# Two more feature tiles in the seven-product groups, and values left without their token scale

## The chip, the core and the metric

The program runs on one core of one Trainium2 chip. Five engines matter: TensorE (PE: matmuls, with PEld for its weight loads), VectorE (DVE), ScalarE (ACT), GpSimd (POOL) and the sync engine (SP), which only issues DMAs here. Every engine takes its own instructions strictly in the order in which the kernel was written and waits on semaphores of the others. The metric is the device time of one execution in microseconds, as the median of the runs of a kernel.

## The reference

The block has a token-mixing half and a feed-forward half, for 256 tokens of width 2048 in float32. The change is in the feed-forward half:

```python
def _rmsnorm(x, g):
    y = xf * lax.rsqrt(jnp.mean(xf * xf, axis=-1, keepdims=True) + EPS)
    return (y * g.astype(jnp.float32)).astype(x.dtype)

def _conv_ffn(h, w_up, dw_w, dw_b, w_down):
    up = h @ w_up
    gate, val = up[..., :D_FF], up[..., D_FF:]
    gate = lax.conv_general_dilated(gate, dw_w, ...) + dw_b
    act = jax.nn.gelu(gate, approximate=False) * val
    return act @ w_down

x = x + _conv_ffn(_rmsnorm(x, norm2_g), w_up, dw_w, dw_b, w_down)
return _rmsnorm(x, normf_g)
```

D_FF is 5504, that is 43 feature tiles of 128. The convolution runs over neighbouring tokens (width 3), for each feature by itself. The last line normalizes every token (row) of x by its own root mean square.

## The kernel before

**Precision.** Every float32 operand of a matmul is split into a high part (`hi`, rounded to the type that TensorE takes in one pass) and the rest (`lo`). ACT makes `hi` by a copy (L197 for weights as loaded, L1129 for the weights of the seven products), DVE makes `lo` by subtracting (L205, L1130). A product is then three matmuls: high by high, high by low, low by high. The `hi` and `lo` buffers of weights are three deep.

**Items.** `ff_items` writes out by hand the order of the feed-forward half, as a list of items. There are 43 gate and 43 value units ("u", written g36 or v36 here for tile 36), each the up-projection of one tile by `still_weights` (L372): 16 matmuls of 512 columns and 16 of 256. There are products ("s"), late downs ("d") and four `last` units. The strings in `PATTERNS` give the order, one string for each group. `ff_step(n)` runs beside item n on PE: it runs the list `beside[n]`, then `split_item(n + 2)`, which splits the weights of the item two further on, and then the list `behind[n]`. What a unit leads to is entered into these lists by `up_posts`: the eviction and sum one item later (`scaled_sum`: ACT copies the low part out of PSUM at L1013, DVE adds at L1015 and multiplies by `r2b`, the row of token scales, at L1016), the convolution (`gate_conv`, L1023 to L1027) and the value product (`val_mult`) two items later.

**The down-projection in three ways.** Tiles in groups go by seven products in place of eight: with the tokens in two halves, the tiles of a group in two halves and the output columns in two halves (n), the 2x2 block product is made from seven block products of sums and differences, named P1, P7, N5, N3, P6, P2, N4, for each of two column blocks c. A group of `(first, m)` holds 2m tiles; each of its 14 products is 3m matmuls of 512 columns (`by_parts`, L1232 to L1234). There are five groups with 36 tiles: one of 4 and four of 8. P1 and N5 gather in four held PSUM banks (`held`) over all groups, P6 and P7 in SBUF tiles `Z` and P2, N3 and N4 in the residual `xs` (`product_out`); `shared_out` adds what is shared at the end, in three steps. Tiles 36 to 39 (`LATE`) are multiplied directly, as four late downs over 512 output columns each (`moving_weights`, L355 to L357); tiles 40 to 42 (`LAST`) come at the end, as eight products of nine matmuls.

In the last group P2 and N4 of each c are not evicted: their banks stay in `joined` until the late down of the same c has added to them, and `down_out` (L1239) adds them to `xs`. The products and units other than the held ones take turns in the four banks of the pool `mm`.

**The weights of the products.** For each group and c four blocks a, b, c, d of the down weights arrive through a ring of two tiles (`rawd`), loaded by SP's queue; the split of P1, P7, N3 and P2 loads the next one. A further tile `x`, called `sumw` in the trace, holds sums: `first_sums` (L1144) makes a + b on DVE, and a DMA that adds while it writes puts d onto b. N5 splits sumw; then such a DMA adds d to it (L1134), P6 splits it; another adds c (L1136), N4 splits it. The adding DMAs are issued by POOL.

**Scales.** `r2b` first holds the two columns of the token norm's reciprocal root; `row_out` turns them and writes them to memory and `row_in` reads them back as a row over all partitions, so that a feature tile (features by tokens) can be multiplied by it. At the end the sums of squares of the residual with EPS give the last norm's scale (`first_squares`, L1245).

Of the kernel before, what the change touches and what calls it, by code (L numbers as in the profile page):

```python
# [11 lines left out]
ALU = mybir.AluOpType  # L12
# [6 lines left out]
NH = 12  # L19
# [7 lines left out]
EPS = 1e-6  # L27
# [14 lines left out]
V_N = 216  # L42
# [35 lines left out]
OUT_ORDER += [(c, k) for c in (2, 3) for k in range(4)]  # L78


GROUPS = [(0, 2), (4, 4), (12, 4), (20, 4), (28, 4)]
LATE = list(range(36, 40))
LAST = list(range(40, NF))
PRODUCTS = [
    ["P1", "P7", "N5", "N3", "P6", "P2", "N4"], ["P1", "N5", "P7", "N3", "P6", "P2", "N4"]
# [1 line left out]


PATTERNS = ["uuu" + "su" * 13 + "s"] * (len(GROUPS) - 1)
PATTERNS += ["uuu" + "su" * 6 + "sdu" + "ssu" * 2 + "suuss" + "ddd"]  # L90


def group_of(j):

    for g, (first, n) in enumerate(GROUPS):
        if j < first + 2 * n:
# [4 lines left out]
def ff_items():  # L101
# [4 lines left out]

    firsts = [first for first, _ in GROUPS] + [LATE[0], NF]
    items = ups(0, firsts[1])
# [12 lines left out]
def block_kernel(  # L121
# [19 lines left out]
    nc = tc.nc  # L141
# [7 lines left out]
    def f32(ap):  # L149
        return ap.bitcast(F32)  # L150
# [5 lines left out]
    units = [(w_u_x[i], 2048) for i in range(4)] + [(w_in[i], 2048) for i in range(20)]  # L156
# [4 lines left out]
    for n, it in enumerate(items):  # L161
        if it[0] == "product":
            continue
        up_index[n] = len(units)
        if it[0] in ("gate", "val"):
            units.append((w_up[2 * it[1] + (it[0] == "val")], 2048))
            shifts.append((0, SHIFT))
            continue
        elif it[0] == "down":
            units.append((w_down_late[it[1]], 2048))  # L170
        else:
            units.append((w_down_last[it[1]], 512 * len(LAST)))
        shifts.append((0, 0))
# [25 lines left out]
    def split_low(i, o=0, n=2048, reload=True):  # L199

        if i >= len(units):
            return
        hi, lo = halves[i]
        s = slice(o, min(o + n, units[i][1]))
        nc.vector.tensor_tensor(lo[:, s], raws[i][:, s], f32(hi[:, s]), ALU.subtract)  # L205
        if s.stop == units[i][1] and reload:
            load(i + RAW)
            load_more(i + RAW)
# [80 lines left out]
    ps = bank(dn, "ps_warm")  # L289
# [3 lines left out]
    def vcol(o, n=1):  # L293
        return vec[:, o : o + n]
# [25 lines left out]
    def row_out(t, name):  # L320

        nc.vector.transpose(t[:, 32:64], t[:, 0:32])
        row = rows.tile([2, 4, 32], F32, tag="row" + name, name="row" + name)
        for b in range(2):
            nc.sync.dma_start(row[b], t[b:P:32, 32:64])
        return row
# [80 lines left out]
    for c in range(4):  # L407
        t = base.tile([P, 4, 512], F32R, tag=f"hT{c}", name=f"hT{c}")
        hT.append(t)
    ps_u = [bank(mm, f"ps_u{b}") for b in range(2)]  # L410
    for k in range(NK):
# [3 lines left out]
        n = 1 if c < 2 else 2  # L415
# [3 lines left out]
        if q % n == 0:  # L419
            w, h = u_part(k, 0, FW, n), hi[:, q : q + n, :]  # L420
# [512 lines left out]
    def flip_x_in(c):  # L933
        t = turned_tiles(c)[1]
        t = st["x", c] = t.rearrange("p (k c) -> p k c", k=4)
        blocks_in(st.pop(("d", "x")), t)
# [19 lines left out]
    for n, (c, kq) in enumerate(OUT_ORDER):  # L956
# [15 lines left out]
        if kq >= 2:  # L972
            part = "a" if kq == 2 else "f"
            ps = ps_a[c] if kq < 3 else ps_a[c, "f"]
# [16 lines left out]
    fp = ctx.enter_context(tc.tile_pool(name="fp", bufs=2))  # L991
    hT[:] = hT2
    r2b = fp.tile([P, S], F32, tag="r2b", name="r2b", bufs=1)
    parts = {}
    gate_out, sums_of, act = {}, {}, {}

# [14 lines left out]
    def scaled_sum(ps, name):  # L1011
        tmp = fp.tile([P, S], F32, tag="ftmp", name=f"ft_{name}")
        nc.scalar.activation(tmp, ps[:, S : 2 * S], AF.Copy)  # L1013
        add = fp.tile([P, S], F32, tag="fadd", name=f"fa_{name}", bufs=3)
        nc.vector.tensor_tensor(add, ps[:, 0:S], tmp, ALU.add)  # L1015
        nc.vector.tensor_tensor(add, add, r2b, ALU.mult)  # L1016
        sums_of[name] = add

    def gate_conv(j):
# [17 lines left out]
    def val_mult(j):  # L1037
        va, ge = sums_of.pop(f"v{j}"), gate_out.pop(j)
        if j >= LATE[0]:
            q = j - LATE[0]  # L1040
            if q % 2 == 0:
# [30 lines left out]
    def block_of(g, name):  # L1072
        k, t = PLACE[name]
        return parts[g, k][:, 0 : GROUPS[g][1], t * P : (t + 1) * P]

    def operand(g, name):

        o = fp.tile([P, 2, 4, P], F32R, tag=f"op_{name}", name=f"op_{name}", bufs=1)
        o = o[:, :, 0 : GROUPS[g][1], :]
        a = block_of(g, name)  # L1080
# [15 lines left out]

    ring, ring_tiles = [(g, c, w) for g in range(len(GROUPS)) for c in range(2) for w in "abdc"], {}
    ring_next = [0]
# [97 lines left out]
    def product_out(g, c, p, ps):  # L1196
        tt = nc.vector.tensor_tensor
        if p in ("P6", "P7"):
            z = Z[c, p]
            if g == 0:  # L1200
                nc.scalar.activation(z, ps, AF.Copy)
            else:
                tt(z, ps, z, ALU.add)
        else:
            n, t = {"P2": (0, 0), "N3": (1, 0), "N4": (0, 1)}[p]
            xb = xs[2 * n + c][:, t, :]
            tt(xb, ps, xb, ALU.add)

    def shared_out(c, step):

        p1, n5, u, p7 = held[c, "P1"], held[c, "N5"], Z[c, "P6"], Z[c, "P7"]
        x00, x10, x01, x11 = (xs[2 * n + c][:, t, :] for n in range(2) for t in range(2))
        tt = nc.vector.tensor_tensor
        if step == 0:
            tt(u, p1, u, ALU.add)
            tt(x00, p1, x00, ALU.add)
            w = st["w", c] = wp.tile([P, 512], F32, tag="junk", name=f"sum01_{c}")
            tt(w, n5, u, ALU.subtract)
        elif step == 1:
            tt(u, u, p7, ALU.add)  # L1220
            tt(x01, x01, st["w", c], ALU.add)
            tt(x10, x10, u, ALU.add)
        else:
            w = st.pop(("w", c))
            tt(w, w, p7, ALU.subtract)
            tt(x11, x11, w, ALU.add)

    def by_parts(ps, o, hi, lo, n, first, last):

# [12 lines left out]
    ssq3 = base.tile([P, 2, 32], F32, tag="ssq3", name="ssq3")  # L1242

    def first_squares(b):
        nc.vector.tensor_scalar(ssq3[:, b, 3:4], ssq3[:, b, 0:1], EPS, None, ALU.add)  # L1245

    ready = {(c, b): xs[c][:, b, :] for c in range(4) for b in range(2)}

# [49 lines left out]
    def last_out_post(c, part, ps):  # L1298

        i = n_front + 2  # L1300
        out_add(c, part, ps)
        flip_x_out(c)
        for o, n in ((0, 512), (512, 1536)):
            split_low(i - 1, o, n)
        out_sums(c)
        split_high(i)
        split_low(i, 0, 1024)
        tot2 = base.tile([P, 2], F32, tag="tot2", name="tot2")
        nc.vector.tensor_reduce(tot2, ssq2, mybir.AxisListType.X, ALU.add)
        rstd_of(tot2, D, "2", r=r2b[:, 0:2])  # L1310
        split_low(i, 1024, 1024, reload=False)
        row = row_out(r2b, "2")
        flip_x_in(c)
        row_in(row, r2b)
        load(i + RAW)
# [4 lines left out]
    for q in range(OPEN):  # L1320
        kind, j = items[q]
        ps = bank(mm, f"ps_{kind}{j}")
# [29 lines left out]
    for n, it in enumerate(items):  # L1352
        if n < OPEN:
            continue
        if it[0] == "last":
            break
        if n in (4, 5):
            ring_load()
        if n == 6:
            pending.append(lambda: first_sums(0, 0))  # L1360
        if it[0] in ("gate", "val"):
            kind, j = it
            ps = bank(mm, f"ps_{kind}{j}")
            still_weights(*halves.pop(up_index[n]), ps, range(NK))
            ff_step(n)
            up_posts(n, kind, j, ps)
            continue
        if it[0] == "product":
            kind, g, c, p = it
            end = g == len(GROUPS) - 1  # L1370
            if (c, p) in held:
                by_parts(held[c, p], parts[p], *halves.pop(it), GROUPS[g][1], g == 0, end)
            elif end and p in ("P2", "N4"):
                ps = joined[c, p] = bank(mm, f"ps_{p}{g}{c}")
                by_parts(ps, parts[p], *halves.pop(it), GROUPS[g][1], True, False)
            else:
                ps = bank(mm, f"ps_{p}{g}{c}")
                by_parts(ps, parts[p], *halves.pop(it), GROUPS[g][1], True, True)
                at(beside, n + 1, product_out, g, c, p, ps)
            if end and p == ("N4", "P6")[c]:  # L1380
                for q in range(3):
                    at(behind, n + 1 + (1 + c) * q, shared_out, c, q)
        else:
            kind, c = it
            hi, lo = halves.pop(up_index[n])
            if c < 2:
                ps = [joined.pop((c, p)) for p in ("P2", "N4")]
            else:
                ps = [bank(mm, f"ps_l{c}{b}") for b in range(2)]
            for b in range(2):  # L1390
                moving_weights(hi, lo, 512, LATE, act.get, b, ps[b], c >= 2, True)
            at(beside, n + 1, down_out, c, ps)
            if c == 1:
                gfb = fp.tile([P, D], F32, tag="sumw", name="gfb", bufs=1)
                nc.gpsimd.dma_start(gfb, normf_g.partition_broadcast(P))
        ff_step(n)
# [165 lines left out]
```

## Time and profile before

| | us |
|---|---|
| median of 3 runs (lowest, highest) | 933.49 (933.27, 934.07) |
| the profiled execution's own time | 933.83 |
| its span in the trace | 932.1 |
| busy in it: PE, DVE, ACT, POOL | 923.2, 776.2, 543.6, 62.8 |

The time of an execution holds a little more than the span from the first to the last instruction in the trace. A row of a group reads: line, engine, operation, output and inputs, shapes, count, then busy time in us and the mean duration of one in ns, then the idle time of the engine before them with what ended it. A row of the timeline starts with the start in us from the span's start and the duration. A row of waits ends with the sum, the count and the longest in us. Matmuls are pipelined, so the distance between the starts of two of them, and not the duration of one, is what it costs.

### The profile page before, as it was taken

The page shows a single profiled execution, that of the slowest core. Times are in us where ns is not written, and L with a number is a line of the kernel's source. Part 1 is how long each engine was busy: PE and PEld are TensorE (multiplying, and loading weights), DVE is VectorE, ACT ScalarE, POOL GpSimd, SP SyncE. Part 2 cuts the span into 40 slices and gives each one's busy share as a digit, 9 for nine tenths or more (in the row PEclk, how much of TensorE's full clock was granted, in tenths as well). Part 3 has the DMA queues.
Part 4 walks back from the last instruction along what each step waited for, and adds up shares of the span by engine and source line. Part 5 has one row for each costly group of instructions (what it writes and reads, how often), then busy time and mean ns, then how long its engine had stood idle before and what let it go on. Part 6 is the DMA issues. An engine that isn't in the chain of part 4 may idle for free.

```text
span 932.1 us, 12883 instructions
## 1 busy us (share of the span) xinstructions
PE 923.2 (99%) x4973; PEld 799.9 (86%) x4973; DVE 776.2 (83%) x997; ACT 543.6 (58%) x689; POOL 62.8 (7%) x79
## 2 busy tenths in 40 slices
PE   9999999999999999999999999999999999999996
PEld 7888998888888888888888888888888888888885
DVE  7768998787768877898877997888978789989995
ACT  6756777546465655565555665555755556655553
POOL 0101111200000000000000000000000000000002
PEclk9999999999999999999999999999999999999999
DMA  9865777667777668788797769887787968779652
GB/s 361 331 225 158 249 241 215 201 198 269 230 274 256 203 207 256 242 274 263 229 299 251 240 209 298 223 260 233 268 240 244 306 221 269 237 238 272 203 180 91
DMA packets 59597, 225.16 MB, mean 242 GB/s; under 512 B 24465, under 2 KB 30225, under 8 KB 35984
## 3 DMA queue, kind: packets, MB, share of 16 engines
q1 hardware_dynamic: 54928, 194.72, 57.9%
q0 software_dynamic: 4464, 29.36, 17.0%
q8 instruction: 39, 0.64, 0.3%
q10 hardware_dynamic: 144, 0.26, 0.1%
q14 instruction: 22, 0.18, 0.0%
HBM read 216.98 MB, written 7.08 MB: 240 GB/s over the span
## 4 chain that ended last, share of the span: by engine, by line
PE 98%; DMA 0%; ACT 0%; DVE 0%; issue 0%; POOLq 0%; POOL 0%; ACTq 0%
PE ps_gate L372 25%; PE ps_val L372 25%; PE ps_q L372 7%; PE ps_P L1233 4%; PE ps_P L1234 4%; PE ps_P L1232 3%; PE ps_N L1233 3%; PE ps_N L1234 3%; PE ps_N L1232 3%; PE ps_k L372 2%; PE ps_a L357 2%; PE ps_a L355 2%; PE ps_a L356 2%; PE ps_s L748 1%; PE ps_o L842 1%; PE ps_ff L355 1%
## 5 line engine op out<-in xcount | busy, mean ns | idle before, releaser
L205 DVE TENSOR_TENSOR lo<-raw,hi 128x2048 fp32r<-128x2048 f32 (+2 forms) x133 | 295.0, 2221 | 28.3 <-ACT hi L197 28.0
L197 ACT ACTIVATE hi<-raw 128x2048 fp32r<-128x2048 f32 (+1 forms) x131 | 246.8, 1887 | 27.6 <-PE ps_a L356 10.8
L372 PE MATMUL ps_gate<-hU,hi 128*128 128x512 f32 x688 | 236.1, 389 | 0.0
L372 PE MATMUL ps_val<-hU,hi 128*128 128x512 f32 x688 | 236.1, 389 | 0.0
L372 PE MATMUL ps_gate<-hU,lo 128*128 128x256 f32 x688 | 189.9, 276 | 0.0
L372 PE MATMUL ps_val<-hU,lo 128*128 128x256 f32 x687 | 189.6, 276 | 0.0
L372 PEld LDWEIGHTS ps_gate<-hU,hi 128*128 128x128 f32 x688 | 129.2, 188 | 26.8
L372 PEld LDWEIGHTS ps_val<-hU,hi 128*128 128x128 f32 x688 | 129.2, 188 | 26.8
L372 PEld LDWEIGHTS ps_gate<-hU,lo 128*128 128x128 f32 x688 | 129.2, 188 | 1.3
L372 PEld LDWEIGHTS ps_val<-hU,lo 128*128 128x128 f32 x687 | 129.0, 188 | 1.3
L1013 ACT ACTIVATE ft_g<-ps_gate 128x256 f32<-128x256 f32 x43 | 16.5, 384 | 121.1 <-PE ps_gate L372 121.1
L1013 ACT ACTIVATE ft_v<-ps_val 128x256 f32<-128x256 f32 x43 | 16.5, 383 | 87.0 <-PE ps_val L372 87.0
L372 PE MATMUL ps_q<-hT,hi 128*128 128x512 f32 x192 | 65.0, 391 | 0.0
L1232 PE MATMUL ps_P<-hi_P,op_P 128*128 128x512 f32 x144 | 56.0, 389 | 0.0
L1233 PE MATMUL ps_P<-hi_P,op_P 128*128 128x512 f32 x144 | 56.0, 389 | 0.0
L1234 PE MATMUL ps_P<-lo_P,op_P 128*128 128x512 f32 x144 | 56.0, 389 | 0.0
L372 PE MATMUL ps_q<-hT,lo 128*128 128x256 f32 x192 | 51.2, 277 | 0.0
L1130 DVE TENSOR_TENSOR lo_N<-sumw,hi_N 128x2048 fp32r<-128x2048 f32 (+1 forms) x20 | 41.5, 2076 | 9.4 <-ACT hi_N L1129 9.2
L1232 PE MATMUL ps_N<-hi_N,op_N 128*128 128x512 f32 x108 | 42.0, 389 | 0.0
L1233 PE MATMUL ps_N<-hi_N,op_N 128*128 128x512 f32 x108 | 42.0, 389 | 0.0
L1234 PE MATMUL ps_N<-lo_N,op_N 128*128 128x512 f32 x108 | 42.0, 389 | 0.0
L372 PEld LDWEIGHTS ps_q<-hT,hi 128*128 128x128 f32 x192 | 35.2, 188 | 6.6
(415 smaller groups left out, 1592.4 us busy)
## 6 DMA issues: line engine op xcount, KB each, us to landing
raw<-in_w_up SPq DMA_DIRECT2D x86, 1024.0 KB, 6.6
raw<-in_w_in SPq DMA_DIRECT2D x20, 1024.0 KB, 5.4
raw<-in_w_out SPq DMA_DIRECT2D x16, 1024.0 KB, 5.1
sumw<-in_w_down POOLq DMA_DIRECT2D x16, 1024.0 KB, 8.6
raw<-in_w_down_late SPq DMA_DIRECT2D x4, 1024.0 KB, 6.8
raw<-in_w_down_last SPq DMA_DIRECT2D x4, 768.0 KB, 4.0
turnp<-flip SPq DMA_DIRECT2D x44, 64.0 KB, 1.9
flop<-turnp SPq DMA_DIRECT2D x11, 256.0 KB, 3.9
```

The lines of the kernel that those rows point to most:

```text
L197: nc.scalar.activation(halves[i][0][:, s], raws[i][:, s], AF.Copy)
L205: nc.vector.tensor_tensor(lo[:, s], raws[i][:, s], f32(hi[:, s]), ALU.subtract)
L355: nc.tensor.matmul(ps, ah, wh, start=first and q == q0, stop=False)
L356: nc.tensor.matmul(ps, al, wh, start=False, stop=False)
L357: nc.tensor.matmul(ps, ah, wl, start=False, stop=last and q == q0 + len(kk) - 1)
L372: nc.tensor.matmul(ps[:, x], (hi, lo)[i][:, k * P : (k + 1) * P], hk(k)[:, x], start=n == 0 and k == 0, stop=n == len(order) - 1 and k == ...
L748: nc.tensor.matmul(ps[:, b * S : (b + 1) * S], qT[:, qo + b * P : qo + (b + 1) * P], kT[:, ko : ko + S], start=n == 0, stop=n == 2,)
L1013: nc.scalar.activation(tmp, ps[:, S : 2 * S], AF.Copy)
L1130: nc.vector.tensor_tensor(lo, src, f32(hi), ALU.subtract)
L1232: nc.tensor.matmul(ps, o[:, 0, p, :], hi[:, s], start=first and p == 0, stop=False)
L1233: nc.tensor.matmul(ps, o[:, 1, p, :], hi[:, s], start=False, stop=False)
L1234: nc.tensor.matmul(ps, o[:, 0, p, :], lo[:, s], start=False, stop=last and p == n - 1)
```

## The change

38 tiles go through the groups: the first group has 6 tiles in place of 4, so that all later groups begin two tiles on, and the late set has two tiles in place of four, with late weights of 1024 columns in place of 2048. The last group's pattern has fewer units, and its products come two at a time from the start. The gate keeps its multiplication by `r2b`, the values lose theirs. So what the down-projection gives is larger by the token's root mean square (`rms2`, the reciprocal of the scale); the residual is multiplied by `rms2` when the first group's products are added to it (one of its four parts in `shared_out`), and EPS of the last norm is multiplied by its square (`eps3`), so that the last norm, which takes out any factor of a token, gives the same. The ring's first loads and the first sums begin at items 8, 9 and 10 in place of 4, 5 and 6.

```diff
-GROUPS = [(0, 2), (4, 4), (12, 4), (20, 4), (28, 4)]
-LATE = list(range(36, 40))
+GROUPS = [(0, 3), (6, 4), (14, 4), (22, 4), (30, 4)]
+LATE = list(range(38, 40))
...
 PATTERNS = ["uuu" + "su" * 13 + "s"] * (len(GROUPS) - 1)
-PATTERNS += ["uuu" + "su" * 6 + "sdu" + "ssu" * 2 + "suuss" + "ddd"]
+PATTERNS += ["uuu" + "ssu" * 3 + "sdu" + "ssu" * 3 + "s" + "ddd"]
...
-            units.append((w_down_late[it[1]], 2048))
+            units.append((w_down_late[it[1]], 512 * len(LATE)))
...
+    rms2, eps3 = vcol(V_N + NH, 2), vcol(V_N + NH + 2, 2)
...
         nc.vector.tensor_tensor(add, ps[:, 0:S], tmp, ALU.add)
-        nc.vector.tensor_tensor(add, add, r2b, ALU.mult)
+        if name[0] == "g":
+            nc.vector.tensor_tensor(add, add, r2b, ALU.mult)
...
-            tt(xb, ps, xb, ALU.add)
+            if g == 0:
+                nc.vector.scalar_tensor_tensor(xb, xb, rms2[:, t : t + 1], ps, ALU.mult, ALU.add)
+            else:
+                tt(xb, ps, xb, ALU.add)
...
-            tt(x11, x11, w, ALU.add)
+            nc.vector.scalar_tensor_tensor(x11, x11, rms2[:, 1:2], w, ALU.mult, ALU.add)
...
-        nc.vector.tensor_scalar(ssq3[:, b, 3:4], ssq3[:, b, 0:1], EPS, None, ALU.add)
+        nc.vector.tensor_scalar(
+            ssq3[:, b, 3:4], ssq3[:, b, 0:1], eps3[:, b : b + 1], None, ALU.add
+        )
...
+        nc.vector.reciprocal(rms2, r2b[:, 0:2])
         row = row_out(r2b, "2")
+        nc.vector.tensor_tensor(eps3, rms2, rms2, ALU.mult)
+        nc.vector.tensor_scalar(eps3, eps3, EPS, None, ALU.mult)
...
-        if n in (4, 5):
+        if n in (8, 9):
             ring_load()
-        if n == 6:
+        if n == 10:
             pending.append(lambda: first_sums(0, 0))
```

## The prediction

> **What bounds the kernel now.** I read the page first, then the waits of TensorE, then its timeline.
>
> ```profile
> span 932.1 us, 12883 instructions
> PE 923.2 (99%) x4973; PEld 799.9 (86%) x4973; DVE 776.2 (83%) x997; ACT 543.6 (58%) x689; POOL 62.8 (7%) x79
> PE 98%; DMA 0%; ACT 0%; DVE 0%; issue 0%; POOLq 0%; POOL 0%; ACTq 0%
> ```
>
> ```profile
> PE ps_warm L291 <- POOL ones L283: 1.0, 1, 1.0
> PE ps_u L429 <- ACT hT L298: 0.2, 1, 0.2
> ```
>
> PE is busy for 99% of the span, carries 98% of the chain that ended last, and after the first microseconds waits for nobody. So a matmul taken away shortens the kernel by its own length, DVE time taken away buys nothing, and any new PE wait is paid in full. The length of a matmul is its pitch, not its modelled duration:
>
> ```profile
> 747.21 0.39 PE L372 MATMUL ps_val<-hU,hi 128*128 128x512 f32 x1
> ...
> 752.65 0.39 PE L1232 MATMUL ps_P<-hi_P,op_P 128*128 128x512 f32 x1
> ...
> 755.37 0.39 PE L372 MATMUL ps_gate<-hU,hi 128*128 128x512 f32 x1
> ```
>
> The first column is the start, the second the modelled duration. An up unit ("u", one gate or value tile) takes 752.65-747.21 = 5.44 us, a four-tile product ("s") 2.72 us for 12 matmuls, so 0.2267 us each.
>
> **The saved matmuls.**
>
> ```profile
> L1232 PE MATMUL ps_P<-hi_P,op_P 128*128 128x512 f32 x144 | 56.0, 389 | 0.0
> L1232 PE MATMUL ps_N<-hi_N,op_N 128*128 128x512 f32 x108 | 42.0, 389 | 0.0
> L355 PE MATMUL ps_l<-hi,act 128*128 128x512 f32 x16 | 6.2, 389 | 0.0
> L1016 DVE TENSOR_TENSOR fa_v<-fa_v,r2b 128x256 f32<-128x256 f32 x43 | 18.3, 425 | 1.5
> ```
>
> Products: (144+108) x 3 lines = 756 matmuls for 36 tiles, 21 a tile. Late: ps_l is half of the column blocks, 16 x 3 = 48, so 96 for 4 tiles, 24 a tile. Two tiles moved: +42-48 = -6 matmuls, **-1.36 us**. The removed value scaling is 18.3 us of DVE; by the waits above it is worth 0 by itself.
>
> **Edits worth nothing.** New small operations and the row of scales:
>
> ```profile
> L787 DVE RECIPROCAL ex<-sm 128x2 f32<-128x2 f32 x12 | 1.9, 155 | 0.0
> L330 SPq DMA_DIRECT2D r2b<-row x1: 332/332/332, 258.0 to 258.0; - x1
> 265.49 0.42 DVE L1016 TENSOR_TENSOR fa_g<-fa_g,r2b 128x256 f32<-128x256 f32 x1
> ```
>
> The reciprocal delays the row's way out by 0.16 us; it is read back at 258.0 and first used at 265.49, which hides it (without that cover: 0.16 us). The two eps3 operations follow the row; eight scalar_tensor_tensor for tensor_tensor cost some 0.06 us each (0.48 against 0.42 in rows below). Group 0 with three tiles has 2.04 us of product to a 5.44 us unit, 7.48; DVE then needs about 2.20+1.66+0.60+1.3 = 5.8, so it stays hidden, as the tighter four-tile groups do now. Ring loads start four items later beside units that start four items later: nothing.
>
> **The new order of the last group.** Before, products and units alternate (s u s u) for its first half c=0. Now two products follow each other: after the last group's own last unit, v37, come N4 (of the group before), g38, v38, g39, P1, P7, v39, N5, N3, g40, P6, P2, v40, N4, down0, g41, P1, N5, v41, P7, N3, g42, P6, P2, v42, N4, down1, down2, down3, last. A down now is 12 matmuls, 2.72 us. So PE has 10.88 us where it had 16.32 from N5 to P6 and from P6 to N4. These three read one tile, sumw: N5 splits it into hi and lo, then POOL's DMA adds d, P6 splits it, a DMA adds c, N4 splits it.
>
> ```profile
> 799.43 2.29 DVE L1130 TENSOR_TENSOR lo_N<-sumw,hi_N 128x2048 fp32r<-128x2048 f32 x1
> ```
>
> ```profile
> 802.01 0.88 POOL L1134 DMA_DIRECT2D sumw<-in_w_down  x1 [29.15 <-DVE lo_N L1130]
> ```
>
> ```profile
> DMA to landing us min/median/max: 8.0/8.5/10.1
> ```
>
> ```profile
> 812.69 0.38 ACT L1013 ACTIVATE ft_v<-ps_val 128x256 f32<-128x256 f32 x1 [2.22 <-PE ps_val L372]
> 812.97 1.91 ACT L1129 ACTIVATE hi_P<-sumw 128x2048 fp32r<-128x2048 f32 x1
> ```
>
> ```profile
> 814.91 2.29 DVE L1130 TENSOR_TENSOR lo_P<-sumw,hi_P 128x2048 fp32r<-128x2048 f32 x1 [0.92 <-ACT hi_P L1129]
> ```
>
> One link, from the end of one lo to PE's start on the next: 0.29 to the issue (801.72 to 802.01), 8.5 landing, 0.05, hi to lo 1.95 (812.97 to 814.91), lo 2.29: **13.08 us**. 16.32 covers it, 10.88 does not. I take the median landing of these last groups; its bounds are 8.0 and 10.1.
>
> DVE's pitches, from stretches where it runs without a gap:
>
> ```profile
> 835.98 2.29 DVE L1144 TENSOR_TENSOR sumw<-rawd41a,rawd41b 128x2048 f32<-128x2048 f32 x1
> 838.18 0.42 DVE L1058 TENSOR_TENSOR act<-fa_v,act 128x256 fp32r<-128x256 f32 x1
> 838.52 0.42 DVE L1015 TENSOR_TENSOR fa_g<-ps_gate,ft_g 128x256 f32<-128x256 f32 x1
> 838.97 0.42 DVE L1016 TENSOR_TENSOR fa_g<-fa_g,r2b 128x256 f32<-128x256 f32 x1
> 839.39 2.29 DVE L205 TENSOR_TENSOR lo<-raw,hi 128x2048 fp32r<-128x2048 f32 x1
> 841.60 0.48 DVE L1024 SCALAR_TENSOR_TENSOR cv<-fa_g,vec,cv 128x255 f32<-128x255 f32 x1
> ...
> 842.52 2.29 DVE L1130 TENSOR_TENSOR lo_P<-rawd41a,hi_P 128x2048 fp32r<-128x2048 f32 x1
> ```
>
> ```profile
> 895.35 2.29 DVE L205 TENSOR_TENSOR lo<-raw,hi 128x2048 fp32r<-128x2048 f32 x1
> 897.55 0.69 DVE L1225 TENSOR_TENSOR sum<-sum,z_P 128x512 f32<-128x512 f32 x1
> 898.27 0.69 DVE L1226 TENSOR_TENSOR xs<-xs,sum 128x512 f32<-128x512 f32 x1
> 898.88 0.68 DVE L1239 TENSOR_TENSOR xs<-ps_P,xs 128x512 f32<-128x512 f32 x1
> ```
>
> ```profile
> L205 DVE TENSOR_TENSOR lo<-raw,hi 128x1536 fp32r<-128x1536 f32 x5 | 8.7, 1754 | 1.2 <-ACT hi L197 1.2
> L205 DVE TENSOR_TENSOR lo<-raw,hi 128x1024 fp32r<-128x1024 f32 x4 | 4.8, 1221 | 0.1
> L1129 ACT ACTIVATE hi_N<-sumw 128x1024 fp32r<-128x1024 f32 x4 | 4.2, 1050 | 0.0
> ```
>
> lo or first sums 2.20; 128x256 steps 0.34 to 0.45 (sum 0.45, gate sum and scale 0.81, conv pair 0.90, act or value product 0.34); 128x512 steps 0.60, a dependent pair 1.32; lo of 1536 and 1024 columns 1.66 and 1.13 (duration less the 0.09 of overlap). A lo behind a unit's eviction starts 2.43 us after the unit: 0.20 (tail of a matmul, 0.39-0.23, and a semaphore), 0.28 and 1.95. PE starts 0.05 after the lo it needs. An item's split is issued two items ahead and its buffer frees three items back.
>
> I set PE's clock to 0 where v37 starts and carry it on.
> (a) **N5 to P6.** g39 ends at 24.48. lo v39 starts at 26.91; then 2.20, operand sums 1.32, operand N5 0.60, act 0.34, conv 0.90, lo N5 2.29: ready at 34.56, due at 35.36. P6 is ready at 34.56+13.08 = 47.64 and due at 46.24: **1.40** (0.46 of it shows before g40, whose lo waits in the same queue: from lo N5's start at 32.27 come 2.20+0.60+0.60+2.20+0.60+0.45+2.29+0.05 = 41.26, due 40.80).
> While ACT waits for sumw, hi P2, the eviction of g40, hi v40 and conv 40 are queued behind it, and on DVE their partners.
> **P6 to N4.** P6's lo had ended at 47.59: N4 is ready at 60.67, due at 47.64+10.88 = 58.52: **2.15**.
> (b) **DVE behind the late N4.** From lo N4's start at 58.33 DVE has in its queue: lo N4 2.20, down0's lo 1.13, first sums 2.20, sum of v40 0.45, lo g41 2.20, value product 0.34, lo P1 2.20, act 0.34, three shared steps 1.80, two down additions 1.20, lo N5 2.20, three more shared steps 1.80, gate sum and scale 0.81, lo v41 2.29: 21.16, v41 ready at 79.54. PE is through N4, down0, g41, P1, N5 at 60.67+16.32 = 76.99: **2.55**, most of it before v41.
> (c) **down2's bank.** c=1 has a unit more between N5 and P6, so that link fits. v41 ends at 84.98; P6's lo ends 2.43+2.20+0.34+0.60+2.29 later, 92.84; N4 is ready at 105.92 and due at 95.86+10.88 = 106.74, 0.82 to spare. But its lo starts only at 103.58, and before the bank is free DVE does lo N4 2.20, shared steps 1.80, lo down1 1.13, sum 0.45, lo down2 1.13, shared steps 1.80, value product 0.34, lo down3 1.13, act 0.34 and the first down addition 0.69: 114.59. Of the four mm banks, down2's second is the one that P2 of c=1 held until that addition (before, it was down3's first). PE reaches it at 106.74+2.72+2.72+1.36 = 113.54: **1.10**.
> (d) **Last units.** From 114.50 DVE does the other down addition 0.60, lo of last0 1.66, the dependent pair 1.32, down2's additions 1.20 and lo of last1 1.75, done at 121.03, due at 120.76 (114.64+1.36+2.72+2.04): 0.32 with the 0.05; then last2 1.66, down3's additions 1.20 and last3 1.75 from 119.28+1.66, done at 125.55 against 125.16 (121.08 and two products of nine matmuls, 2.04 each): 0.44. Together **0.76**.
>
> Sum of waits 1.40+2.15+2.55+1.10+0.76 = 7.96; less 1.36: **+6.60 us**. Other DMAs moved: d and c of c=0 are asked for by SP after the lo of P1 and P7 (about 18 and 24) and read at 33 and 45; POOL's addition to b goes out near 6.8 and P7 reads at 19.5, 12.7 us for a landing of 10.1 at most: hidden. POOL has nothing else in its queue there.
>
> The same chain worked for before, with 16.32 us per link, gives no wait, as the trace has none. DVE was near its limit even so:
>
> ```profile
> 774.00:801.00 27.00, 27.00 (x153) 23.59 (x152) 25.80 (x33) 17.79 (x21) 0.00 (x0) 1.00 0.76 250
> ```
>
> 25.80 of 27.00 us (fourth column) in this group's first stretch. The profiled execution took 933.83 us (span 932.1), 0.3 us over the median 933.49; the sum goes on the median: **940.1 us**.
>
> **Rivals.** A: **sumw lands in time**, not slower by the measure. If a landing takes 6.35 us or less (13.08-8.5+6.35 = 10.93, less 0.05), no link holds PE. For it: a plain ring load of this size landed in 6.0:
>
> ```profile
> rawd41b<-in_w_down SPq DMA_DIRECT2D x1, 1024.0 KB, 6.0
> ```
>
> Against it: no addition to sumw here landed under 8.0. Left are 0.46 at g40, 1.34 at v41 (v40's end + 2.43, then b's list from lo g41 on, 15.18, and 0.05, against 16.32 of PE), 0.25 at the bank (v42's end, 0.48 and 1.09 to down2's lo, then 1.13+1.80+0.34+1.13+0.34+0.69+0.05, against 2.72+2.72+1.36) and 0.76: 2.81, net +1.45, **934.9**. The Trainium skill (DMA: Bandwidth & Descriptors, Anatomy of one DMA) fits GpSimd-issued transfers with 2.0 us plus bytes over 436 GB/s, an estimate of 4.4 us for 1 MiB; by that the sum would be this rival's. The trace does not agree: 8.0 to 10.1.
>
> B: **the count alone**. PE stays without a gap, -1.36, **932.1**. It decides only if besides A's landing DVE takes up A's other 2.81 us too, 1.34 of them over five items; 25.80 of 27.00 speaks against that.
>
> C: **landings at the upper bound**, 10.1, since DMAs are packed closer. Each 0.1 costs 0.3 (two links, and the bank by way of N4): 7.96+4.8 = 12.8, net +11.4, **944.9**. For it: the 10.1 happened, at half the density of products. Against: the landing quoted above for N5 to P6 belongs to a stretch with DVE and DMA as full as this one will be. The Trainium skill (SBUF — State Buffer, SBUF: two separate sides) warns that a GpSimd-issued DMA can be starved of descriptors while VectorE holds the port that they share; here the issue took 0.88 us beside a nearly gapless DVE, so no run here shows it.
>
> **Chances.** Forecast 0.75, C 0.09, A 0.08, B 0.05, and 0.03 for a gain over 0.2% from something unseen. A measurement here tells 0.2% (1.87 us) from no change; A and B lie within it. So slower 0.84, same 0.13, faster 0.03. The range reaches from A's 934.9 to C's 944.9; the forecast's own is 938.6 (landing 8.0: 7.96-1.5-1.36 = +5.1) to 941.9 (landing 9.1, +8.4).
>
> **What would show it.** Right: 798 product and 48 late matmuls; PE waits for lo_P and lo_N with ACT's hi waiting for the landing in sumw, about 3.5 us over two places of the last group, 2.5 about v41, 1 at ps_l. The first three quarters of the feed-forward keep 8.16 us per pair. Wrong: PE without waits (B), waits on DVE alone (A), or waits in group 0 or at the opening, which nothing above foresees.

## The result, and the profile after

The changed kernel took **943.96 us** (median of 4 runs, 943.12 to 944.73) against 933.38 (933.25 to 934.07) for the kernel before on the same chip: a ratio of **1.011, 95% interval 1.0094 to 1.0126**, slower. The forecast was 940.1. A later group of runs of the same changed kernel, told below, gave 942.06 and a ratio of 1.0082 (1.0062 to 1.0101). Some executions of the kernel before and of experiments 1, 5, 7 and 8 took some 16 us longer, at the same granted clock (0.996 to 0.999); they are left out, and the medians below are of the others.

The profiled execution took 944.18 us. From its page: the span, the busy times, the chain that ended last and two groups of product matmuls.

```profile
span 942.4 us, 12827 instructions
...
PE 925.5 (98%) x4967; PEld 798.0 (85%) x4967; DVE 763.4 (81%) x955; ACT 545.5 (58%) x687; POOL 62.5 (7%) x79
...
PE 80%; DVE 7%; DMA 7%; issue 3%; ACT 2%; SPq 1%; POOL 0%; POOLq 0%; DVEq 0%; ACTq 0%
...
L1239 PE MATMUL ps_P<-lo_P,op_P 128*128 128x512 f32 x152 | 59.4, 391 | 0.9 <-DVE lo_P L1132 0.8
...
L1239 PE MATMUL ps_N<-lo_N,op_N 128*128 128x512 f32 x114 | 44.5, 390 | 1.2 <-DVE lo_N L1132 1.2
```

PE has six matmuls fewer (4967 against 4973), (152 + 114) x 3 = 798 of them in products, and DVE 12.8 us less work. But PE's share of the chain fell from 98% to 80%: DVE, DMA and the issue of instructions now stand on the path. Who PE waited for, in the view of its waits (sum, count, longest):

```profile
PE ps_val L372 <- DVE lo L205: 2.8, 3, 1.7
PE ps_e L1422 <- DVE lo L205: 1.6, 2, 0.9
PE ps_N L1239 <- DVE lo_N L1132: 1.2, 1, 1.2
PE ps_warm L291 <- POOL ones L283: 1.0, 1, 1.0
PE ps_P L1239 <- DVE lo_P L1132: 0.8, 1, 0.8
PE ps_gate L372 <- DVE lo L205: 0.3, 1, 0.3
```

Every new wait is for a low half made by DVE. The view counts the idle time of PE alone; what is lost is the distance between the starts of two matmuls less the pitch of 0.2267 us. PE's timeline around the last group's first P6 and N4:

```profile
843.26 0.40 PE L1238 MATMUL ps_P<-hi_P,op_P 128*128 128x512 f32 x1
844.49 0.50 PE L1239 MATMUL ps_P<-lo_P,op_P 128*128 128x512 f32 x1 [0.83 <-DVE lo_P L1132]
844.83 0.39 PE L1237 MATMUL ps_P<-hi_P,op_P 128*128 128x512 f32 x1
...
856.17 0.39 PE L1238 MATMUL ps_N<-hi_N,op_N 128*128 128x512 f32 x1
857.76 0.50 PE L1239 MATMUL ps_N<-lo_N,op_N 128*128 128x512 f32 x1 [1.19 <-DVE lo_N L1132]
```

The two matmuls with the high weights run at once and the third, the first that reads the low half, waits: 844.49 - 843.26 - 0.23 = 1.00 us, and 0.11 more to the next start, 1.11 for P6. Added up in this way over the whole timeline, PE loses:

| place | changed kernel, first profile | second profile | forecast |
|---|---|---|---|
| second unit's value at the opening, 252 us | 1.46 | 0 | 0 |
| g40, P6 (and P2, v40 behind it), N4 of c=0 | 0.25, 1.11, 0.83, 1.46 | 0.25, 1.24, 0.83, 1.27 | 3.55 in all |
| g41, v41 | 0.57, 1.98 | 0.63, 1.95 | 2.55 |
| late downs | 0.15 | 0.29 | 1.10 |
| last units | 2.16 | 2.12 | 0.76 |

The kernel before loses nothing after its first microseconds. Behind the last matmul there is one more loss, in what is called the drain below. The span before ended 8.0 us after the start of the last matmul (924.08 to 932.1), here 9.1 (933.29 to 942.4): +1.1.

The links of the chain by way of sumw are on POOL's and ACT's timelines, POOL's issue of the adding DMA and ACT's first read of what it wrote:

```profile
831.28 0.88 POOL L1136 DMA_DIRECT2D sumw<-in_w_down  x1 [25.56 <-DVE lo_N L1132]
844.73 0.88 POOL L1138 DMA_DIRECT2D sumw<-in_w_down  x1 [12.58 <-DVE lo_P L1132]
```

```profile
840.19 1.92 ACT L1131 ACTIVATE hi_P<-sumw 128x2048 fp32r<-128x2048 f32 x1 [6.04 <-DMA sumw<-in_w_down]
853.46 1.92 ACT L1131 ACTIVATE hi_N<-sumw 128x2048 fp32r<-128x2048 f32 x1 [4.47 <-DMA sumw<-in_w_down]
```

From issue to first read are 8.91 and 8.73 us, and ACT stands still for the last 6.04 and 4.47 of them. Then DVE, from the late N4 on, has no gap (its timeline, rows left out between):

```profile
855.41 2.29 DVE L1132 TENSOR_TENSOR lo_N<-sumw,hi_N 128x2048 fp32r<-128x2048 f32 x1 [3.34 <-ACT hi_N L1131]
857.62 1.22 DVE L205 TENSOR_TENSOR lo<-raw,hi 128x1024 fp32r<-128x1024 f32 x1
858.75 2.28 DVE L1146 TENSOR_TENSOR sumw<-rawd41a,rawd41b 128x2048 f32<-128x2048 f32 x1
...
871.55 0.68 DVE L1225 TENSOR_TENSOR z_P<-z_P,z_P 128x512 f32<-128x512 f32 x1
...
874.15 2.29 DVE L205 TENSOR_TENSOR lo<-raw,hi 128x2048 fp32r<-128x2048 f32 x1
```

The row at 874.15 is the low half of v41. PE's wait for it ended at 876.49, 21.08 us after 855.41; the list worked out in the prediction gave 21.16 plus 0.05.

### The profile page after: what moved, and what is told of

Its sections match the earlier page's. It is cut to its first block, busy times and chain, and to the rows that moved or that the text cites. A ratio compares the mean times of both kernels' runs of the same rounds, so it can differ in the third digit from the quotient of the medians.

```text
span 942.4 us, 12827 instructions
## 1 busy us (share of the span) xinstructions
PE 925.5 (98%) x4967; PEld 798.0 (85%) x4967; DVE 763.4 (81%) x955; ACT 545.5 (58%) x687; POOL 62.5 (7%) x79
## 4 chain that ended last, share of the span: by engine, by line
PE 80%; DVE 7%; DMA 7%; issue 3%; ACT 2%; SPq 1%; POOL 0%; POOLq 0%; DVEq 0%; ACTq 0%
PE ps_val L372 23%; PE ps_gate L372 23%; PE ps_q L372 7%; PE ps_P L1237 3%; PE ps_P L1239 3%; PE ps_P L1238 3%; DMA sumw<-in_w_down 3%; PE ps_k L372 2%; PE ps_N L1237 2%; PE ps_N L1239 2%; PE ps_N L1238 2%; DVE lo L205 2%; PE ps_s L748 1%; PE ps_o L842 1%; PE ps_a L357 1%
## 5 line engine op out<-in xcount | busy, mean ns | idle before, releaser
L205 DVE TENSOR_TENSOR lo<-raw,hi 128x2048 fp32r<-128x2048 f32 (+2 forms) x133 | 290.7, 2188 | 31.3 <-ACT hi L197 30.8
L197 ACT ACTIVATE hi<-raw 128x2048 fp32r<-128x2048 f32 (+2 forms) x131 | 243.5, 1860 | 25.2 <-PE ps_a L356 9.9
L1239 PE MATMUL ps_P<-lo_P,op_P 128*128 128x512 f32 x152 | 59.4, 391 | 0.9 <-DVE lo_P L1132 0.8
L1237 PE MATMUL ps_P<-hi_P,op_P 128*128 128x512 f32 x152 | 59.2, 389 | 0.0
L1238 PE MATMUL ps_P<-hi_P,op_P 128*128 128x512 f32 x152 | 59.1, 389 | 0.0
L1132 DVE TENSOR_TENSOR lo_N<-sumw,hi_N 128x2048 fp32r<-128x2048 f32 (+1 forms) x20 | 43.6, 2182 | 18.7 <-ACT hi_N L1131 18.7
L1239 PE MATMUL ps_N<-lo_N,op_N 128*128 128x512 f32 x114 | 44.5, 390 | 1.2 <-DVE lo_N L1132 1.2
L1238 PE MATMUL ps_N<-hi_N,op_N 128*128 128x512 f32 x114 | 44.4, 389 | 0.0
L1237 PE MATMUL ps_N<-hi_N,op_N 128*128 128x512 f32 x114 | 44.3, 389 | 0.0
L1131 ACT ACTIVATE hi_N<-sumw 128x2048 fp32r<-128x2048 f32 (+1 forms) x20 | 36.5, 1824 | 7.8 <-DMA sumw<-in_w_down 7.8
```

Of the source, the lines that this page charges most:

```text
L197: nc.scalar.activation(halves[i][0][:, s], raws[i][:, s], AF.Copy)
L1131: nc.scalar.activation(hi, src, AF.Copy)
L1132: nc.vector.tensor_tensor(lo, src, f32(hi), ALU.subtract)
L1237: nc.tensor.matmul(ps, o[:, 0, p, :], hi[:, s], start=first and p == 0, stop=False)
L1238: nc.tensor.matmul(ps, o[:, 1, p, :], hi[:, s], start=False, stop=False)
L1239: nc.tensor.matmul(ps, o[:, 0, p, :], lo[:, s], start=False, stop=last and p == n - 1)
```

## The experiments

Each is an edit of the changed kernel, but for the first, which is an edit of the kernel before, and the last, which has no edit. All ratios are to the kernel before.

**1. The values without their scale, alone.** The edits of `r2b`, `rms2` and `eps3` on the kernel before, the groups, patterns and late weights of which stay.

```diff
-        nc.vector.tensor_tensor(add, add, r2b, ALU.mult)
+        if name[0] == "g":
+            nc.vector.tensor_tensor(add, add, r2b, ALU.mult)
...
```

> The kernel before, with the values unscaled and the residual multiplied (the rms2 and eps3 part of the change alone; groups, pattern and ring as before). Theory (the loss sits in the new order of the last group, the scale part is worth nothing): 933.4 us, between 932.8 and 934.2, TensorE without a wait after the first microseconds. Rival 1 (the scale part lengthens the path of the row of token scales and costs the 1.6 us that TensorE lost near 251 us in the trace after): 935.0 us, with that wait in the trace.

Measured: 933.88 us, ratio 0.9998 (0.9988 to 1.0008). Its PE waits after the opening of the program are none; the view holds one row:

```profile
PE ps_warm L291 <- POOL ones L283: 1.0, 1, 1.0
```

DVE is busy 759.5 us in place of 776.2, and that buys nothing. The new operations cost nothing either.

**2. The two more tiles, alone.** The changed kernel with values scaled as before, and without `rms2` and `eps3`.

```diff
-        if name[0] == "g":
-            nc.vector.tensor_tensor(add, add, r2b, ALU.mult)
+        nc.vector.tensor_tensor(add, add, r2b, ALU.mult)
...
```

> The changed kernel with the values scaled as before (38 tiles in groups, new pattern, no rms2 and eps3). Theory: the order costs what it costs, the 0.36 us of DVE that comes back for each value adds a little where DVE is behind: 944.3 us, between 943.3 and 945.5. Rival 1 (the scale part costs 1.6): 942.4 us. Rival 2 (the removed scaling is what kept the new order from being much worse): over 946 us.

Measured: 943.12 us, ratio 1.0101 (1.0088 to 1.0115), 0.2 us under the expected range. PE loses 8.74 us at the same places, with no loss at the opening. The whole slowdown belongs to the tiles and the order.

**3. Without the DMAs that add to sumw in the last group.** sumw keeps a + b for all three products.

```diff
         if p in ("P1", "P7", "N3", "P2"):
             ring_load()
+        elif g == len(GROUPS) - 1 and p in ("N5", "P6"):
+            pass
         elif p == "N5":
```

> The changed kernel without the two DMAs that add to sumw in each half of the last group (P6 and N4 of that group use the sum as N5 left it). Theory (the landing of these additions, 8.6 to 8.8 us in the trace, is what makes P6 and N4 late, and DVE's queue behind them is late for it): the waits at P6 and N4 of the first half vanish, some 1.1 us at v41 and 1.8 at the last units stay, 937.1 us, between 936 and 938.5. Rival 3 (DVE's own work in the new order is the bound and the landing only hides it): 941 us or more, with TensorE waiting at the same places for as long.

Measured: 935.82 us, ratio 1.0025 (1.0015 to 1.0034), 0.2 us under the expected range. Of the waits for low halves one is left, at v41:

```profile
PE ps_val L372 <- DVE lo L205: 0.9, 1, 0.9
```

So some 6 to 8 us of the loss (942.06 or 943.96, less 935.82) hang on two transfers for each c. The edit takes away their traffic with their landing; but experiments 4 and 5 keep the transfers and lose the waits, so that it is the waiting for them that costs. PE loses 2.08 us, where the prediction's rival A had 2.81: 0.25 at g40 (0.46), 1.15 at v41 (1.34), nothing at the bank (0.25) and 0.67 at last units (0.76). The drain of 9.1 us is in this run too (925.26 to 934.4).

**4. The last group in another order.** The units stand elsewhere between the products. For c=0 the link from P6 to N4 has 16.32 us of PE again (835.42 to 851.74). The one from N5 to P6 still has 10.88 (824.54 to 835.42), not the 13 that the expectation names; but N5's low half is made earlier, as told under (a) below.

```diff
-PATTERNS += ["uuu" + "ssu" * 3 + "sdu" + "ssu" * 3 + "s" + "ddd"]
+PATTERNS += ["usuussussusussususssdsuusddd"]
```

> The changed kernel with another pattern for the last group, usuussussusussususssdsuusddd: the units stand so that N5 to P6 and P6 to N4 are at least 13 us apart on TensorE and fewer units come first. Theory: no wait is left but some 0.8 us before last3; the six matmuls are saved: 932.8 us with the opening as in the trace before, 934.4 us with the 1.6 us lost there as in the trace after. Rival 3 (DVE is the bound in this group with ten units, however they stand): 938 us or more. Rival 4 (the loss comes with 38 tiles, whatever the pattern): 943 us.

Measured: 935.08 us, ratio 1.0015 (1.0006 to 1.0024), over the 932.8 that was expected. The waits for low halves are gone and a new one stands in their place, for a PSUM bank. P2 and N4 of c=0, both waiting for their late down, keep two of the four `mm` banks, and a product comes to the bank of an earlier one whose addition into `z_P` stands in DVE's queue behind a low half made from sumw:

```profile
PE ps_P L1237 <- DVE z_P L1205: 1.6, 1, 1.6
```

DVE's timeline has that low half and the addition behind it; the product starts at 877.99:

```profile
874.62 2.29 DVE L1132 TENSOR_TENSOR lo_P<-sumw,hi_P 128x2048 fp32r<-128x2048 f32 x1 [1.65 <-ACT hi_P L1131]
...
877.16 0.68 DVE L1205 TENSOR_TENSOR z_P<-ps_P,z_P 128x512 f32<-128x512 f32 x1
```

**5. The order with the banks freed sooner.** The downs in the order 0, 2, 1, 3, and down0 earlier.

```diff
-PATTERNS += ["uuu" + "ssu" * 3 + "sdu" + "ssu" * 3 + "s" + "ddd"]
+PATTERNS += ["usuussussusussudsusssduussdd"]
...
-            "d": [("down", c) for c in range(4)],
+            "d": [("down", c) for c in (0, 2, 1, 3)],
```

> As e4_spread, with down0 five items earlier and down2 before the last products (pattern usuussussusussudsusssduussdd, downs in the order 0, 2, 1, 3), so that the banks of P2 and N4 of the first half come free before the second half's products need them. Theory (the one wait left in e4_spread, 1.77 us before a product's first matmul with z_P's addition as releaser, is a PSUM bank held back by those two): that wait goes, 933.3 us, between 932.7 and 934.0, TensorE losing under 0.8 us. Rival (a wait of DVE's queue and not of the bank): 935 us, the wait stays or moves.

Measured: 934.23 us, ratio 1.0002 (0.9991 to 1.0012), 0.2 us over the expected range. PE waits for nobody after the first microseconds and loses 0.36 us before one last unit. The order alone takes back the whole slowdown. But the time is not 1.36 us under that of before: the drain is 9.1 us here too (last matmul at 923.70, span 932.8).

**6. Without the shared sums of c=0.** `shared_out` is not run for c=0.

```diff
-            if end and p == ("N4", "P6")[c]:
+            if end and c > 0 and p == ("N4", "P6")[c]:
```

> The changed kernel without the three shared steps of the first half (its P1, N5 and their sums are left out of the result): 4.9 us of DVE less behind the late N4. Theory: the 1.97 us lost before v41 vanish, the 4.6 us lost before it stay: 942.0 us, between 941.2 and 942.8. Rival (the wait at v41 is the landing again and not DVE's queue): 943.5 or more.

Measured: 941.13 us, ratio 1.0077 (1.0062 to 1.0092), 0.1 us under the expected range. The wait at v41 is gone, those for P6 and N4 are as they were, and PE loses 5.65 us in place of 8.69 (the first profile without its opening). The view of waits:

```profile
PE ps_N L1239 <- DVE lo_N L1132: 1.2, 1, 1.2
PE ps_e L1422 <- DVE lo L205: 1.0, 2, 0.6
PE ps_P L1239 <- DVE lo_P L1132: 0.7, 1, 0.7
```

So v41's wait is for room in DVE's queue and not for its weights.

**7. The shared sums of c=0 five items later**, on two occasions.

```diff
-                    at(behind, n + 1 + (1 + c) * q, shared_out, c, q)
+                    at(behind, n + 1 + (1 + c) * q + 5 * (c == 0), shared_out, c, q)
```

> The changed kernel with the three shared steps of the first half five items later. Theory (DVE is full over the whole second half, so what leaves v41 comes back further on): the wait at v41 goes and one of about the same size turns up at P2, N4 or v42 of the second half: 943.6 us, between 942.8 and 944.6. Rival (the lack of DVE time is local to v41): 942.0 us, and no new wait.

> The changed kernel with the shared sums of column block 0 five items later, for a look at where PE waits. Theory (the sums stand in the queue ahead of the low half of v41): no wait at v41, and the time that is won there partly lost at the items to which the sums were moved, a wait of 1 to 2 us between 885 and 915 us; 942.0 to 943.6 us. Rival (v41 waits for late weights alone): the wait at v41 stays at 2 us, 944 us.

Measured: 941.30 and 942.98 us, ratio 1.0088 (1.0068 to 1.0108) from these two runs, then 942.80. The time alone would not decide: the mean of the first two lies under the theory's range, near the rival's 942.0. PE's timeline of the later profile shows v41 without a wait and two new ones:

```profile
893.66 0.50 PE L1239 MATMUL ps_P<-lo_P,op_P 128*128 128x512 f32 x1 [1.09 <-DVE lo_P L1132]
...
898.04 0.38 PE L372 MATMUL ps_val<-hU,lo 128*128 128x256 f32 x1 [1.57 <-DVE lo L205]
```

The wait moved with the sums: 1.36 and 1.85 us at P6 and v42 of c=1, for 1.98 at v41 and nothing at these two. Five items on, DVE's queue has no more room for them than it had.

**8 and 9. The drain.** The addition of last unit 0 (token tile 0) in front of the low half of last unit 3, on experiment 5 and on the changed kernel.

```diff
             run(beside, n0)
-            split(i + 3)
+            split_high(i + 3)
+            last_post(c, b, ps, o, n)
+            split_low(i + 3)
             run(behind, n0)
-        last_post(c, b, ps, o, n)
+        else:
+            last_post(c, b, ps, o, n)
```

> The kernel with the late steps spread and the banks freed in order, and beside that the addition of last unit 0 of token tile 0 is put on VectorE ahead of the split's low half of last unit 3. Theory: the loss after the last matmul (9.1 us against 8.0) comes from that addition, which stood behind a low half whose weights land late, so that GpSimd's three products with the final gains came 2 us late and ran beside VectorE's sum of squares; the reading before had the first product at 914.3 less 1.7, so here it begins about 2 us earlier, the drain is 8.0 to 8.3 us and the time 932.8 (932.2 to 933.5), just under the kernel before. Rival: the drain is set by something else (the broadcast of the gains, the store queues), it stays at 9.1, and the time at 933.7 to 934.5.

> The changed kernel with the addition of last unit 0 of token tile 0 ahead of the low half of last unit 3, and nothing else. Theory: the drain falls from 9.1 to 8.0 us, the low half behind it begins about 0.4 us later, so that last unit 3 waits 0.4 us more: 943.2 us (942.5 to 943.7). Rival, that the drain is set elsewhere: 944.0 to 944.4.

Measured: 933.56 us, ratio 0.9995 (0.9986 to 1.0005), and 941.49, ratio 1.0082 (1.0066 to 1.0098). The first lies just over the upper bound that was expected. The drains are 7.9 (923.86 to 931.8) and 8.0 us (932.39 to 940.4), as expected. What had made them long is in the changed kernel's timelines of DVE and of POOL:

```profile
924.89 1.87 DVE L1265 TENSOR_TENSOR xs<-ps_e,xs 128x512 f32<-128x512 f32 x3
926.80 1.51 DVE L1276 CUSTOM_DVE_ANT_0 z_P<-xs,ssq 128x512 f32<-128x512 f32 x1
```

```profile
924.81 1.29 POOL L1260 TENSOR_TENSOR xs<-xs,gfb 128x512 f32<-128x512 f32 x1 [20.77 <-ACT junkc L1269]
926.46 3.00 POOL L1260 TENSOR_TENSOR xs<-xs,gfb 128x512 f32<-128x512 f32 x2 [0.36 <-ACT junkc L1269]
929.42 0.57 POOL L1288 TENSOR_TENSOR rstd<-ssq,half_pow 128x1 f32<-128x1 f32 x1
```

The same view of POOL for the kernel before:

```profile
912.46 1.29 POOL L1253 TENSOR_TENSOR xs<-xs,gfb 128x512 f32<-128x512 f32 x1 [26.23 <-ACT junkc L1262]
...
918.07 0.57 POOL L1281 TENSOR_TENSOR rstd<-ssq,half_pow 128x1 f32<-128x1 f32 x1 [1.11 <-DVE ssq L1274]
```

The first product on POOL starts 8.48 us ahead of the last matmul (933.29), and 11.62 before the change (924.08), since the addition it needs (at 923.28) stood behind a low half whose weights were late. So `rstd`, behind POOL's products, starts 3.87 us ahead of the last matmul and not 6.01. DVE waits for it and begins the last sum of squares 2.03 us after the start of the last matmul (935.32), and not 0.89 (924.97): the 1.1 us of the drain. With the addition in front, in experiment 8:

```profile
913.10 1.98 POOL L1260 TENSOR_TENSOR xs<-xs,gfb 128x512 f32<-128x512 f32 x1 [16.82 <-ACT junkc L1269]
...
918.50 0.57 POOL L1288 TENSOR_TENSOR rstd<-ssq,half_pow 128x1 f32<-128x1 f32 x1
```

That is 5.36 us before its last matmul, which is enough: the last sum of squares follows that by 0.89 us again (924.75). The time of 941.49 lies 1 us under the expected range; the expectation had the 1.46 us at the opening in it, which this execution does not show.

Experiment 8 is the best order with 38 tiles that was found, and it is level with the kernel before: PE has 1.36 us less to do, loses 0.48, and ends 0.22 sooner (923.86 against 924.08). So 0.66 us of the gain are missing. Of these, 0.22 lie ahead of the feed-forward half: PE starts the first gate at 246.94, and at 246.71 in the kernel before (the profiles of all kernels here have 246.2 to 247.2). The other 0.45 lie between 860 and 890 us, where many distances between the starts of matmuls are some 0.01 us above the pitch; why they are is open. A lower clock it is not: from 300 to 740 us both kernels have a mean of 0.2267 us for 512 columns.

**10. The changed kernel once more**, for a second profile.

> The changed kernel as it is, once more, for a second profile of it. Theory (the 1.5 us that PE lost at 252 us came from transfers that landed late in that one execution, since no other profile with the same instructions there has it): no wait of PE between 240 and 830 us, a span of about 941 us in the profile, and a median of 942.8 to 944.0. Rival (unscaled values cost it, through the rows of the norm that are turned there): the wait at 252 us is there again, the span is 942.4.

Measured: 942.06 us (941.5 to 942.4), span 940.6, no wait of PE between 240 and 830 us. ACT's timeline at the opening, first of the first profile, then of this one:

```profile
244.83 1.71 ACT L947 ACTIVATE hU<-flipx2lo,vec 128x256 fp32r<-128x256 f32 x4 [7.09 <-DMA flipx2lo<-turnx]
```

```profile
241.87 1.71 ACT L947 ACTIVATE hU<-flipx2lo,vec 128x256 fp32r<-128x256 f32 x4 [4.43 <-DMA flipx2lo<-turnx]
```

The same read of turned rows waited 2.66 us longer in the first. It was a transfer of that execution, not the change: neither this one nor experiment 1, which has the same scales, shows it. How many of the unprofiled first runs had it stays open. The median came 0.7 us under the lower bound that was expected.

## Why the forecast was right, and where its steps were not

**The saved matmuls**: six, as said.

**The values' scale, worth nothing**: shown by experiments 1 and 2.

**(a) the links by sumw**: 3.55 us forecast up to N4, 3.65 and 3.59 found. P6's first matmul with a low half came 13.51 us after the low half of N5 ended (828.70 + 2.28 to 844.49), where 13.08 had been taken; the landing is 8.9 in place of 8.5 with the start of the read. Experiment 3 shows that the additions carry it, experiments 4 and 5 that the order does. But PE's 10.88 us in place of 16.32 is not the whole of it. Experiments 4 and 5 give PE its 16.32 us back from P6 to N4 of c=0 alone; from N5 to P6 they leave it 10.88, and still there is no wait. The time that counts runs from the end of the first low half, and that comes earlier in them. DVE's low half of N5 and PE's start on N5, first in the changed kernel, then in experiment 4:

```profile
828.70 2.28 DVE L1132 TENSOR_TENSOR lo_N<-sumw,hi_N 128x2048 fp32r<-128x2048 f32 x1
831.76 0.39 PE L1237 MATMUL ps_N<-hi_N,op_N 128*128 128x512 f32 x1
```

```profile
818.84 2.28 DVE L1132 TENSOR_TENSOR lo_N<-sumw,hi_N 128x2048 fp32r<-128x2048 f32 x1
824.54 0.39 PE L1237 MATMUL ps_N<-hi_N,op_N 128*128 128x512 f32 x1
```

The low half ends 0.78 us ahead of N5 in the changed kernel (the sum had 0.80) and 3.42 in experiment 4. With 10.88 us from N5 to P6 in both, that makes 11.66 us in the changed kernel, too few for the link, and 14.30 in experiment 4, enough.

**(b) DVE's queue behind the late N4**: 2.55 us forecast, 2.55 and 2.58 found. The list of the prediction is DVE's list in the trace, step by step, and experiment 6 shows that the shared sums are what v41 stands behind.

**(c) down2's bank, 1.10 us**: wrong. The sentence that failed is that "down2's second is the one that P2 of c=1 held". PE's and DVE's timelines of the changed kernel:

```profile
910.41 0.39 PE L355 MATMUL ps_l<-hi,act 128*128 128x512 f32 x1
...
911.55 0.39 PE L357 MATMUL ps_l<-lo,act 128*128 128x512 f32 x1
911.93 0.47 PE L355 MATMUL ps_l<-hi,act 128*128 128x512 f32 x1
```

```profile
911.10 0.69 DVE L1244 TENSOR_TENSOR xs<-ps_P,xs 128x512 f32<-128x512 f32 x1
```

down2's second bank is written from 910.41, before the addition of 911.10 reads P2. The first matmul to come behind that addition is that of 911.93, down3's first: 1.36 us later than I had it due, so 0.15 us is lost and 0.29 in the second profile. It starts 0.14 us after the addition's end, as the product of experiment 4 that waits for a bank starts 0.15 us after its own. That a bank can hold PE in this kernel is shown by experiment 4.

**(d) the last units, 0.76 us**: right in kind, short by 1.4. I had DVE's queue late and the weights there. The late queue also issues the loads late, since a load waits for the low half three units back, and then the weights land late. SP's issues, before and after:

```profile
890.78 11.40 SPq L181 DMA_DIRECT2D raw<-in_w_down_last  x4
```

```profile
906.12 8.28 SPq L181 DMA_DIRECT2D raw<-in_w_down_last  x4
```

The second column is the time over which the four went out. The first load goes out 17.0 us ahead of last unit 0 before (907.76) and 8.6 after (914.75). Part of that is the order itself, with downs of half the length: experiment 3, in the same order without the late additions, has 10.4 (897.74 to 908.14), and loses 0.67 us there. Before, what ended ACT's idle time ahead of its four high halves was PE wherever it was idle, and never a transfer; after, it is the landing each time. Two of the four in ACT's timeline:

```profile
916.84 1.49 ACT L197 ACTIVATE hi<-raw 128x1536 fp32r<-128x1536 f32 x1 [1.92 <-DMA raw<-in_w_down_last]
...
920.08 1.49 ACT L197 ACTIVATE hi<-raw 128x1536 fp32r<-128x1536 f32 x1 [1.76 <-DMA raw<-in_w_down_last]
```

Their median landing is 5.7 us, and 4.0 before.

**The drain**, 1.1 us, was not in the sum at all: the forecast ended at PE's last matmul. Experiments 8 and 9 show its cause.

**The sum** for the second profile: -1.36 + 6.17 + 0.29 + 2.12 + 1.1 = 8.3, with the span 8.5 us longer (940.6 against 932.1). The forecast's +6.60 lacked 1.4 at the last units and 1.1 in the drain, and had 0.8 too much at the bank. The first profile has the 1.46 of the opening on top. Both medians, 943.96 and 942.06, lie above the 938.6 to 941.9 that the forecast gave its own mechanism. That the first lies in the stated range is luck in part: the range reached up to rival C, and C did not happen.

**The rivals.** A (the landing hidden) and B (the count alone) fell with landings of 8.9 and 8.7. C had the time nearest to the first median, 944.9, but not by its mechanism: no landing near 10.1 stood in these links. The Trainium skill's fit for GpSimd-issued transfers (DMA: Bandwidth & Descriptors, Anatomy of one DMA) gives an estimate of 4.4 us for 1 MiB. The adding transfers here do not agree: they took twice that, 8.6 to 8.9 us to land, as they had before.

## What to carry to other kernels

Before work is packed closer, follow every chain through a single buffer that is read, changed by a transfer and read again: its length doesn't shrink with the work beside it, here 13.3 to 13.5 us. Set against it the time from the end of the first read to the need of the last, 11.7 us at N5 here, and not only the work between them; an earlier first read covers it too. An engine's queue that is late also issues its loads late, so a delay in the middle is paid again at the end, once in late weights and once in the drain; carry a forecast to the last instruction and not to the last matmul. Work taken off an engine that is not on the critical path (here 17 us of DVE) was worth nothing, in the old order (experiment 1) as in the new one (experiment 2).

## What the runs showed of the hardware beside this

POOL's product and a DVE operation with both inputs in SBUF hold each other up. POOL's product of 128x512 takes 1.29 us; beside DVE's additions out of PSUM (924.81 in the changed kernel) it still does. In experiment 8 it starts at 913.10 while DVE makes a low half, and takes 1.98:

```profile
912.18 1.75 DVE L205 TENSOR_TENSOR lo<-raw,hi 128x1536 fp32r<-128x1536 f32 x1
```

That is 0.69 us longer, about the 0.83 us for which the low half still ran. In the changed kernel DVE's sum of squares starts at 926.80, after POOL's second product began, and takes 1.51 us in place of the 0.75 that it takes in the kernel before and in experiment 8. (In experiment 8 it starts 0.2 us ahead of the end that the trace gives for POOL's second product, and is not held up; POOL's spans are rough.) The Trainium skill (SBUF — State Buffer, SBUF: two separate sides) says that the pair of ports that the two share is locked for a whole instruction by whichever starts first; these rows agree.
